# ScalarE held to the written order where an encoder's gates get their first two combinations

## The chip, the cores and the metric

The kernel runs on one core of a Trainium2 chip. The metric is device time in microseconds of one execution; less is better. The engines are named as in the profile: PE (TensorE, the matmuls; PEld is its weight load), DVE (VectorE), ACT (ScalarE), POOL (GpSimd) and SP (SyncE), the last two mostly issuing DMAs here.

## What is computed

A bidirectional encoder trunk of two layers on 512 tokens of width 1024, in float32:

```
for l in range(2):
    x = x + 0.5 * swiglu(rms_norm(x), ffn1)
    h = rms_norm(x)
    q, k, v, uf, ga, gf = split(h @ w_in)
    y_na = neighbourhood_attention(q, k, v, rpb) @ w_na_out
    y_f  = real(fft2(uf per group)) @ w_f_out
    x = x + (sigmoid(ga + b0) * y_na + sigmoid(gf + b1) * y_f) @ w_o
    x = x + 0.5 * swiglu(rms_norm(x), ffn2)
return rms_norm(x)
```

The change lies in the mixer, where the products for the gates `ga` and `gf` begin.

## The kernel before

**Float32 out of two halves.** Every matrix is split into a high part `hi` (rounded by ACT) and a low part `lo` (what is left, by DVE). A product is then three matmuls: L280 takes `hi` of both sides, L281 and L282 one `lo` and one `hi` each. The helper `split` (L284 to L290) issues the ACT instruction (L286) and the DVE instruction (L287). Weights of 128x1024 float32 go through the same split, in `Item.prep`, into tiles `whi` and `wlo`, three buffers each; a weight that is needed with its sign turned is split at L172 (ACT) and L173 (DVE).

**The stream of weights.** All weights stand in one list in the order of their use. `ws.next()` hands out the next one, and first has those prepared that lie up to two further on; `ws.prep(n)` prepares up to place n. Their loads into `raw` tiles run eight items ahead, on SP's queue. In the gates some weights are sums of matrices: POOL's queue issues a DMA that adds a second matrix to a `raw` tile, at L152 ahead of the first use and at L179 between two uses.

**Seven products for eight.** A block of the gate products follows Strassen's scheme. `gate_block` runs the products in the order 1, 5, 2, 6, 7, 3, 4. Products 1, 6, 7 and 4 go to the PSUM pair `A`, 5 and 3 to `B`, 2 to `C`. The weight `d` serves products 5, 6 and 3, with another matrix added between them. On the side of the activations the products need combinations of the four quarters `B[i, j]` of the normalised input, which itself is held as `xh` and `xl`:

- `t1` = quarter (0,0) less (0,1), for product 5: `minus` (two subtractions, L1088, and an addition, L1089), then `split` into `t1h` (ACT) and `t1l` (DVE).
- `t2` = `t1` plus quarter (1,1), for product 6: two additions in place at L1097, then `split` into `t2h` and `t2l`.
- `third` and `fourth` make the two others later, while the gate products run; `fourth` changes the tile of `t1` again and writes into the second half of `xh` and `xl`.

**The section.** Ahead of the gate products stands the product of the attention's output `o` with its weights: `fill(o, ns, 0)` takes two weights, and for each of four blocks of 128 tokens it issues twelve matmuls into a PSUM bank `ps` (`rows_of`) and a copy to `fs` on ACT (L943). It is a generator, which yields after each block.

**What sets the order.** The kernel is written for a scheduler that orders each engine's instructions by itself. Inside `tc.manual_schedule(engines=...)` the named engines keep the order in which the code is written; the others stay free. Each engine then runs its own list strictly in that order, and a buffer that is still in use makes the instruction that wants it wait, with all that is queued behind it on its engine. Before the change the section names DVE alone. So DVE has, in this order: three weights' `wlo`, the three steps of `t1`, `t1l`, the two additions, `t2l`, and the `wlo` of the second gate weight (L173), which the `ws.next()` inside `fill` brings. The scheduler put ACT's `whi` of the second gate weight (L172) and of the third (L286) ahead of `t1h`, and the fourth ahead of `t2h`.

```
def split(hi, lo, src, scale=None):
    if scale is None:
        S.activation(hi, src, AF.Copy)
        V.tensor_tensor(lo, src, hi.bitcast(F32), ALU.subtract)
def parts(src, s):
    h, l = slot(F32R, s + "h"), slot(F32R, s + "l")
    split(h, l, src)
    return h, l, 0
```

Of the kernel before, what the change touches and what calls it, by code (L numbers as in the profile page):

```python
# [92 lines left out]
def encoder_kernel(  # L93
# [19 lines left out]
    def slot(dt=F32, s="k", shape=(4, 256)):  # L113
        return kp.tile([P, *shape], dt, tag="k", name=nm(s), bufs=23)
# [129 lines left out]
    class Stream:  # L244
# [25 lines left out]
        def next(self):  # L270
            self.prep(self.pos + 1 + AHEAD)
            it = self.items[self.pos]
            self.pos += 1
            return it.out

    ws = Stream()
# [149 lines left out]
# [4 lines that stand above are left out]
# [246 lines left out]
    def stage_mixer(l, norm, nxt):  # L676
# [15 lines left out]
        for hl in range(2):  # L692
            for c in range(2):
                G.dma_start(out=dfs[c][hl], in_=dft[hl, c])
            src = bass.AP(tensor=rot.tensor, offset=rot.offset + hl * T, ap=[[0, P], [1, T]])
# [121 lines left out]
        o, q, k, bms = [], {}, {}, {}  # L817
# [106 lines left out]
        def rows_of(src, tb, w):  # L924

            ps = bank()
            t = slice(tb * P, (tb + 1) * P)
            for kt, (h_, l_) in enumerate(src):
                wh, wl = w[kt // 2]
                c = slice((kt % 2) * T, (kt % 2 + 1) * T)  # L930
                mm3(ps, h_[:, t], l_[:, t], wh[:, c], wl[:, c], kt == 0, kt == 3)
            return ps

        fs, ns = {}, {}

        def fill(src, to, i):

            w = [ws.next(), ws.next()]
            for tb in range(TB):
                if tb % 2 == 0:  # L940
                    to[i, tb // 2] = slot(F32, "fs", (2, T))
                ps = rows_of(src, tb, w)
                S.activation(to[i, tb // 2][:, tb % 2, :], ps, AF.Copy)  # L943
                yield
# [116 lines left out]
        def f_rows():  # L1061
            for i in range(2):
                yield from fill(yf, fs, i)
# [11 lines left out]
        for which in range(2):  # L1075
            b_ = slot(F32, "gb", (D,))
            src = bass.AP(tensor=gbias.tensor, offset=gbias.offset + (2 * l + which) * D, ap=[[0, P], [1, D]])
# [7 lines left out]
        def minus(p, q, s):  # L1085
            t, u = slot(F32, s), slot(F32, s)
            for z, d in enumerate((t, u)):
                V.tensor_tensor(d, p[z], q[z], ALU.subtract)  # L1088
            V.tensor_tensor(t, t, u, ALU.add)  # L1089
            return t  # L1090

        with tc.manual_schedule(engines={mybir.EngineType.DVE}):
            ws.prep(ws.pos + 3)
            t12 = minus(B[0, 0], B[0, 1], "t1")
            acts[5] = parts(t12, "t1")
            for z in B[1, 1]:
                V.tensor_tensor(t12, t12, z, ALU.add)  # L1097
            acts[6] = parts(t12, "t2")
            n_fill = fill(o, ns, 0)
            next(n_fill)  # L1100
        for _ in n_fill:
            pass

        def third():
# [13 lines left out]
        w = [ws.next(), ws.next()]  # L1118
# [71 lines left out]
    for kt in range(DT):  # L1190
        src = slot(F32, "xt", (T,))
# [9 lines left out]
    for l in range(L):  # L1201
        nxt = Norm(3 * l + 1)
        stage_ffn(norm, nxt, False)
        norm, nxt = nxt, Norm(3 * l + 2)
        stage_mixer(l, norm, nxt)
        norm, nxt = nxt, Norm(3 * l + 3)
        stage_ffn(norm, nxt, l == L - 1)
        norm = nxt
# [130 lines left out]
```

## Time and profile before

| | |
|---|---|
| time, median of 3 runs | 1957.36 us (1956.55 to 1959.98) |
| the profiled execution | 1960.45 us, its span 1958.0 us |
| PE busy | 1918.9 us (98%) |
| PEld busy | 1585.9 us (81%) |
| DVE busy | 1616.4 us (83%) |
| ACT busy | 1121.0 us (57%) |
| POOL busy | 198.3 us (10%) |
| moved by DMA | 361.82 MB, mean 185 GB/s |

Times in the views count from the start of the span. Busy shares are means over stages with different limits, so what the section is worth is read from its own stretch: around 490 to 560 us in layer 0, and 1461 to 1530 us in layer 1. A row's text "out<-in" names the tiles; the number in square brackets is the idle time of the engine ahead of the instruction, with what ended it.

### The profile page before, as it was taken

How to read it: one execution, taken by the hardware profiler on the slowest of the kernel's cores; microseconds unless marked ns; L12 is line 12 of the kernel's file. 1: busy time of each engine (PE TensorE's matmuls, PEld its weight loads, DVE VectorE, ACT ScalarE, POOL GpSimd, SP SyncE). 2: the span in 40 equal slices, each digit the busy share in tenths (PEclk: the TensorE clock that was granted, in tenths of full speed). 3: DMA queues.
4: the chain of work that ended last, by engine and by line, in shares of the span. 5: the costliest groups of instructions: out<-in, count | busy, mean ns of one | idle time of the engine just before them, and what ended most of it. 6: DMA issues, size and time to landing. Idle time of an engine off the chain costs nothing.

```text
span 1958.0 us, 24573 instructions
## 1 busy us (share of the span) xinstructions
PE 1918.9 (98%) x8997; PEld 1585.9 (81%) x8997; DVE 1616.4 (83%) x1936; ACT 1121.0 (57%) x1594; POOL 198.3 (10%) x242
## 2 busy tenths in 40 slices
PE   8999999999899999999999999999998999999997
PEld 6888887888778888888788888878887888888885
DVE  7778899598779877889977878995877888787898
ACT  6555666455556655566555556653555666555663
POOL 0001010200111000101000100102101110010010
PEclk9999999999999999999999999999999999999999
DMA  8677499221997567749757765984039974776593
GB/s 293 186 201 193 147 264 321 72 61 58 239 221 203 133 188 204 185 152 262 226 141 194 198 177 167 278 267 114 18 103 231 238 185 134 207 183 172 172 282 121
DMA packets 105704, 361.82 MB, mean 185 GB/s; under 512 B 12016, under 2 KB 14192, under 8 KB 105584
## 3 DMA queue, kind: packets, MB, share of 16 engines
q1 hardware_dynamic: 78576, 266.92, 39.9%
q0 software_dynamic: 27008, 93.34, 26.2%
q8 instruction: 70, 1.15, 0.2%
q14 instruction: 50, 0.41, 0.1%
HBM read 354.97 MB, written 2.10 MB: 182 GB/s over the span
## 4 chain that ended last, share of the span: by engine, by line
PE 83%; DVE 10%; DMA 3%; issue 2%; ACT 2%; SPq 0%; DVEq 0%; POOL 0%; ACTq 0%; POOLq 0%
PE A L281 8%; PE A L282 8%; PE A L280 8%; PE o L281 5%; PE o L282 5%; PE o L280 5%; PE B L281 4%; PE B L282 4%; PE B L280 4%; PE ps L281 4%; PE ps L282 4%; PE ps L280 4%; DVE wlo L287 3%; DMA raw<-in_wst_dram 2%; PE C L281 2%
## 5 line engine op out<-in xcount | busy, mean ns | idle before, releaser
L287 DVE TENSOR_TENSOR wlo<-raw,whi 128x1024 fp32r<-128x1024 f32 (+1 forms) x522 | 620.9, 1196 | 259.2 <-ACT whi L286 258.0
L286 ACT ACTIVATE whi<-raw 128x1024 fp32r<-128x1024 f32 (+1 forms) x522 | 540.4, 1038 | 513.8 <-PE A L282 130.2
L152 POOL DMA_DIRECT2D raw<-in_wst_dram x152 | 131.2, 874 | 1343.3 <-DMA raw<-in_wst_dram 898.1
L281 PE MATMUL A<-wlo,xh 128*128 128x512 f32 x384 | 152.0, 396 | 12.9 <-DVE wlo L173 12.4
L170 DVE TENSOR_TENSOR raw<-raw,raw 128x1024 f32<-128x1024 f32 (+1 forms) x128 | 150.9, 1189 | 2.4
L282 PE MATMUL A<-whi,xl 128*128 128x512 f32 x384 | 151.2, 394 | 0.0
L280 PE MATMUL A<-whi,xh 128*128 128x512 f32 x384 | 150.0, 392 | 0.4 <-ACT whi L172 0.4
L172 ACT ACTIVATE whi<-raw 128x1024 fp32r<-128x1024 f32 x76 | 78.8, 1038 | 85.7 <-PE B L282 33.2
L173 DVE SCALAR_TENSOR_TENSOR wlo<-raw,whi 128x1024 fp32r<-128x1024 f32 x76 | 89.8, 1193 | 13.5 <-ACT whi L172 13.5
L281 PEld LDWEIGHTS A<-wlo,xh 128*128 128x128 f32 x384 | 73.1, 190 | 30.2 <-DVE wlo L173 14.1
L436 ACT ACTIVATE sn<-A 128x512 f32<-128x512 f32 x96 | 57.3, 598 | 52.1 <-PE A L282 52.0
L282 PEld LDWEIGHTS A<-whi,xl 128*128 128x128 f32 x384 | 73.2, 191 | 15.1
L280 PEld LDWEIGHTS A<-whi,xh 128*128 128x128 f32 x384 | 72.6, 189 | 15.9 <-ACT whi L172 0.8
L281 PE MATMUL B<-wlo,t1h 128*128 128x512 f32 x192 | 75.4, 393 | 1.3 <-DVE wlo L287 1.2
L280 PE MATMUL B<-whi,t1h 128*128 128x512 f32 x192 | 76.1, 398 | 0.1
L280 PE MATMUL A<-whi,t2h 128*128 128x512 f32 x192 | 75.1, 391 | 0.0
L282 PE MATMUL B<-whi,t1l 128*128 128x512 f32 x192 | 75.1, 391 | 0.0
L280 PE MATMUL C<-whi,xh 128*128 128x512 f32 x192 | 75.0, 390 | 0.0
L280 PE MATMUL A<-whi,t3h 128*128 128x512 f32 x192 | 74.9, 390 | 0.0
L281 PE MATMUL C<-wlo,xh 128*128 128x512 f32 x192 | 74.8, 390 | 0.0
L281 PE MATMUL A<-wlo,t3h 128*128 128x512 f32 x192 | 74.7, 389 | 0.0
L281 PE MATMUL A<-wlo,t2h 128*128 128x512 f32 x192 | 74.7, 389 | 0.0
(336 smaller groups left out, 4917.8 us busy)
## 6 DMA issues: line engine op xcount, KB each, us to landing
raw<-in_wst_dram SPq DMA_DIRECT2D x462, 512.0 KB
raw<-in_wst_dram POOLq DMA_DIRECT2D x168, 512.0 KB, 7.8
raw<-in_wst_dram SPq DMA_DIRECT2D x32, 256.0 KB
vs<-v SPq DMA_DIRECT2D x12, 256.0 KB
bw<-in_rpb_dram SPq DMA_DIRECT2D x32, 68.0 KB
xt<-in_xtr_dram SPq DMA_DIRECT2D x8, 256.0 KB
x<-in_xin_dram SPq DMA_DIRECT2D x4, 512.0 KB
raw<-in_wst_dram POOLq DMA_DIRECT2D x8, 256.0 KB, 9.2
```

Source lines behind the costliest of these rows:

```text
L152: G.dma_start(out=self.t, in_=wst[GRAN_AT[self.plus]][:, 0 : self.n], accum_op=ALU.add)
L170: V.tensor_tensor(t, t, self.add.t, ALU.add)
L172: S.activation(hi, t, AF.Copy, scale=-1.0)
L173: V.scalar_tensor_tensor(lo, t, -1.0, hi.bitcast(F32), ALU.mult, ALU.subtract)
L280: PE.matmul(ps, lh, rh, start=start, stop=False, skip_group_check=again)
L281: PE.matmul(ps, lh, rl, start=False, stop=False, skip_group_check=again)
L282: PE.matmul(ps, ll, rh, start=False, stop=stop, skip_group_check=again)
L286: S.activation(hi, src, AF.Copy)
L287: V.tensor_tensor(lo, src, hi.bitcast(F32), ALU.subtract)
L436: S.activation(t[:, b, :], ps[b], AF.Copy)
```

## The change

The section names ACT beside DVE, so ACT's instructions there keep the written order too. The first block's matmuls and copy of `fill` leave the section, and with them go the other three; its two weights are still taken inside it, and handed to `fill`.

```diff
-        def fill(src, to, i):
-
-            w = [ws.next(), ws.next()]
+        def fill(src, to, i, w=None):
+
+            w = w or [ws.next(), ws.next()]
             for tb in range(TB):
...
-        with tc.manual_schedule(engines={mybir.EngineType.DVE}):
+        with tc.manual_schedule(engines={mybir.EngineType.DVE, mybir.EngineType.Activation}):
             ws.prep(ws.pos + 3)
             t12 = minus(B[0, 0], B[0, 1], "t1")
             acts[5] = parts(t12, "t1")
             for z in B[1, 1]:
                 V.tensor_tensor(t12, t12, z, ALU.add)
             acts[6] = parts(t12, "t2")
-            n_fill = fill(o, ns, 0)
-            next(n_fill)
-        for _ in n_fill:
+            w = [ws.next(), ws.next()]
+        for _ in fill(o, ns, 0, w):
             pass
```

## The prediction, made before the result was known

> **What bounds the kernel now.** I read the page first (PE is busy for 98% of the span), then the waits of the stretch from 500 to 640 us, which holds the changed section of layer 0, then the order of time of ACT, DVE and PE there. Each layer runs the section once, and layer 1 repeats layer 0 at 971.29 us later (the difference of two PE rows below, 1484.90 and 513.61).
>
> The waits (engine, line, what it waited for; total us, times, longest):
>
> ```profile
> DVE wlo L287 <- ACT whi L286: 16.4, 10, 4.0
> ...
> ACT whi L172 <- issue: 7.9, 1, 7.9
> ...
> DVE t1l L287 <- ACT t1h L286: 6.5, 1, 6.5
> ...
> PE A L281 <- DVE wlo L173: 6.0, 2, 5.7
> ```
>
> The last row is what counts: PE stands for 5.7 us for one `wlo`. ACT, then DVE, then PE in order of time (start, length, ..., idle before and its releaser):
>
> ```profile
> 494.03 1.05 ACT L172 ACTIVATE whi<-raw 128x1024 fp32r<-128x1024 f32 x1
> 502.98 1.06 ACT L172 ACTIVATE whi<-raw 128x1024 fp32r<-128x1024 f32 x1 [7.90 <-issue]
> 504.29 1.06 ACT L286 ACTIVATE whi<-raw 128x1024 fp32r<-128x1024 f32 x1 [0.25 <-PE ps L282]
> 505.26 1.04 ACT L286 ACTIVATE t1h<-t 128x1024 fp32r<-128x1024 f32 x1
> ...
> 510.11 1.06 ACT L286 ACTIVATE t2h<-t 128x1024 fp32r<-128x1024 f32 x1 [1.99 <-DVE t L1097]
> 511.07 2.04 ACT L943 ACTIVATE fs<-ps 128x512 f32<-128x512 f32 x4
> ...
> 539.79 2.01 ACT L286 ACTIVATE whi<-raw 128x1024 fp32r<-128x1024 f32 x2 [4.20 <-DMA raw<-in_wst_dram]
> ```
>
> ```profile
> 498.65 1.22 DVE L1089 TENSOR_TENSOR t<-t,t 128x1024 f32<-128x1024 f32 x1
> 506.33 1.23 DVE L287 TENSOR_TENSOR t1l<-t,t1h 128x1024 fp32r<-128x1024 f32 x1 [6.46 <-ACT t1h L286]
> ...
> 511.20 1.23 DVE L287 TENSOR_TENSOR t2l<-t,t2h 128x1024 fp32r<-128x1024 f32 x1 [1.12 <-ACT t2h L286]
> 512.34 1.22 DVE L173 SCALAR_TENSOR_TENSOR wlo<-raw,whi 128x1024 fp32r<-128x1024 f32 x1
> 513.48 2.35 DVE L287 TENSOR_TENSOR wlo<-raw,whi 128x1024 fp32r<-128x1024 f32 x2
> ...
> 540.88 1.23 DVE L287 TENSOR_TENSOR wlo<-raw,whi 128x1024 fp32r<-128x1024 f32 x1 [4.03 <-ACT whi L286]
> ```
>
> ```profile
> 506.81 0.62 PE L280 MATMUL A<-whi,xh 128*128 128x512 f32 x2
> 507.27 0.61 PE L280 MATMUL B<-whi,t1h 128*128 128x512 f32 x2
> 513.61 0.79 PE L281 MATMUL A<-wlo,xh 128*128 128x512 f32 x1 [5.73 <-DVE wlo L173]
> ...
> 517.96 0.39 PE L281 MATMUL B<-wlo,t1h 128*128 128x512 f32 x1
> ...
> 522.97 0.39 PE L280 MATMUL C<-whi,xh 128*128 128x512 f32 x1
> ...
> 528.63 0.39 PE L281 MATMUL A<-wlo,t2h 128*128 128x512 f32 x1
> ...
> 542.40 0.39 PE L281 MATMUL B<-wlo,xh 128*128 128x512 f32 x1
> ...
> 545.82 0.50 PE L281 MATMUL A<-wlo,xh 128*128 128x512 f32 x1 [0.53 <-DVE wlo L287]
> ```
>
> DVE has the first combination at 498.65 + 1.22 = 499.87, and ACT is idle then, yet `t1h` starts at 505.26. ACT's queue has two weight splits ahead of it: the `whi` at 502.98 waits for a free buffer until PE has used it up, and the one at 504.29 does too. DVE, held to the written order, stands 6.46 us at `t1l`; behind that stand the two additions, `t2l`, and only then the `wlo` that PE wants at about 507.9. The second half of that price is the clock, told by these stretches (busy us and instructions of PE, PEld, DVE, ACT, POOL, then granted PE clock, DMA share, GB/s):
>
> ```profile
> 511.01:517.83 6.82, 4.22 (x10) 3.35 (x11) 6.63 (x6) 2.70 (x6) 1.71 (x2) 0.50 0.74 159
> 517.83:524.66 6.83, 6.83 (x31) 5.64 (x31) 6.83 (x7) 5.71 (x7) 0.00 (x0) 1.00 0.86 171
> 524.66:539.69 15.03, 15.03 (x68) 12.21 (x67) 10.99 (x12) 6.87 (x9) 2.60 (x3) 1.00 0.94 246
> 1483.80:1490.63 6.83, 5.73 (x14) 4.48 (x15) 6.83 (x7) 2.25 (x5) 1.70 (x2) 0.50 0.72 152
> 954.74:958.15 3.41, 0.95 (x3) 0.30 (x2) 3.41 (x5) 3.02 (x4) 0.00 (x0) 1.00 0.59 171
> 958.15:961.57 3.42, 3.36 (x8) 2.68 (x9) 3.42 (x5) 1.49 (x3) 0.00 (x0) 0.50 0.88 293
> ```
>
> After the stall the clock is at half for 6.82 us in either layer. From 513.61 to 517.96 PE issues ten matmuls, 0.435 us each; from 517.96 to 522.97 twenty-two, 0.228 us each.
>
> **The change part by part.** It adds and removes no instruction; it fixes ACT's order in the section. The order that the program of the changed kernel has, engine by engine: ACT does `whi` of the first gate weight (494.03), `t1h`, `t2h`, then `whi` of the second (502.98 before), the four `fs` copies, and the two `whi` of B's weights. DVE keeps its order up to the second gate weight's `wlo`, then takes the two steps of `fourth` ahead of B's two `wlo`. PE does B's first two matmuls after all of A instead of ahead of A's last ten. SP's and POOL's orders are as before, so no DMA passes another.
>
> *The chain to A's last weight, layer 0.* `t1h` starts on DVE's release: 499.90 (a hand-over between the two engines takes 0.03 us: 505.26 + 1.04 to 506.33). That is 5.36 us earlier. From there the same work at the same lengths: `t1l` 506.33 - 5.36 = 500.97, `t2h` 504.75, `t2l` 505.84, `wlo` 506.98. The `whi` that it needs is now the late one: it stands behind `t2h`, starts 0.96 us after it (511.07 - 510.11) at 505.71 instead of 502.98, and ends at 506.77. PE wants it at 506.81, so its delay of 2.73 us costs nothing, but with 0.04 us of cover; each us that `t2h` came later would cost PE one. PE's `wlo` matmul follows the `wlo` by 513.61 - 512.34 = 1.27 us: 508.25, against 513.61.
>
> *A's rest and B.* Ten matmuls of A at 0.228 us end at 510.53, if the clock stays whole; two of B follow, to 510.99. B's first `wlo` now has two steps of DVE ahead of it at 1.14 us each (512.34 to 513.48 is such a step): 506.98 + 3 x 1.14 = 510.40, usable at 511.67. Its `whi` comes after the four `fs` copies, 506.67 + 2.04 = 508.71 to 509.77, in time. So a new, smaller wait of 0.68 us stands there; the second `wlo` (usable at 512.81) is early for 513.95. B's other 22 matmuls take 5.02 us, and C starts at 516.69 against 522.97: **6.28 us** earlier in layer 0. In the split of it, 5.36 comes from the wait and the rest, 0.92, from the whole clock less the new wait and the two matmuls that moved behind.
>
> Layer 1, PE and then DVE:
>
> ```profile
> 1484.90 0.79 PE L281 MATMUL A<-wlo,xh 128*128 128x512 f32 x1 [5.73 <-DVE wlo L173]
> ...
> 1494.96 0.39 PE L280 MATMUL C<-whi,xh 128*128 128x512 f32 x1
> ...
> 1514.43 0.39 PE L281 MATMUL B<-wlo,xh 128*128 128x512 f32 x1
> ```
>
> ```profile
> 1510.62 1.23 DVE L287 TENSOR_TENSOR wlo<-raw,whi 128x1024 fp32r<-128x1024 f32 x1 [1.78 <-ACT whi L286]
> ```
>
> There C started at 1494.96, which is 523.67 on layer 0's scale, because the half clock covered more matmuls; against 516.69 the gain is **6.98 us**.
>
> *Does C find its weights?* DVE goes on without a hole: two `wlo` of B, two steps of `third`, then C's `wlo` at 510.40 + 4 x 1.14 = 514.96, usable at 516.23; C wants it at 516.69 + 2 x 0.228 = 517.15. The cover is 0.9 us.
>
> *What is late next: the weights made by adding DMAs.* `d` is used three times in a block, and between the uses POOL's queue adds another matrix to it.
>
> ```profile
> 515.22 0.85 POOL L179 DMA_DIRECT2D raw<-in_wst_dram  x1 [7.05 <-DVE wlo L287]
> ...
> 529.27 1.22 POOL L179 DMA_DIRECT2D raw<-in_wst_dram  x1
> ```
>
> In layer 0 the last of these additions, issued at 529.27, held ACT 4.20 us until 539.79 and made the `wlo` at 540.88 (done 542.11) for the matmul at 542.40: 0.29 us of cover. PE now wants it 6.28 us earlier. How much earlier it lands is unknown; bounds: if issue and landing follow DVE's shift, 5.36 us; if only the DMA engines' idle time can be filled, 0.26 x 6.82 + 0.14 x 6.83 + 0.06 x 15.03 = 3.6 us (the first three stretches above). With 5.36 the layer keeps 5.36 + 0.29 = 5.65 us, with 3.6 it keeps 3.9. I take the middle, 4.5 us earlier, so 4.8 us kept. In layer 1 the same `wlo` is done at 1511.85 for 1514.43, a cover of 2.58 us: with 4.5 us all 6.98 are kept, with 3.6 it is 6.2.
>
> **Sum:** 4.8 + 7.0 = 11.8 us. The profiled execution took 1960.45 us (span 1958.0 and 2.45 around it), so it would take 1948.6; the median of the runs, 1957.36, becomes 1945.6 (0.60% less). PE is the bound behind the section (`cl` of the next stage follows it), so the rest of the kernel only shifts.
>
> **A rule that speaks against it.** In the trace one stretch of 3.41 us with PE busy for 0.95 of it (954.74) is followed by half clock for 3.42 us. The changed section has two short holes, from about 507.4 to 508.25 and from 511.1 to 511.67, so any stretch of 3.41 us has at most 1.4 us of idle time, 2.0 us busy. The Trainium skill, "TensorE: Matmul & The Clock Gate", Part 1: the HAM clock gate, has the clock halved after an idle window of about 3.4 us; by it the holes are harmless and 1945.6 stands, though the trace's row at 954.74 shows that a window need not be wholly idle. The same page, under "A second HAM failure mode", tells of a kernel whose frequent micro-idles between groups of matmuls made the clock swing; by that the time would be the first rival's.
>
> **The rivals.**
> 1. *The clock falls all the same.* The two holes, 0.57 us of work between them and the next, drop it for 6.82 us in each layer with PE at work: 2 x 6.82 / 2 = 6.8 us lost, gain 5.0, 1952.4. Against it: 2.0 us busy of 3.41 is twice the 954.74 stretch's share. Chance 0.06.
> 2. *DMA is the bound.* The added matrices land when they landed before. Layer 0 keeps nothing (PE waits for 542.11 as before), layer 1 keeps its cover of 2.58 us: 1954.8. For it: the share of 0.94 ahead of 539.69. Against it: 0.74 and 0.86 in the stretches ahead, idle because the requests that free buffers and finished `wlo` send were late too. Chance 0.09.
> 3. *Slower: an addition blocks ACT.* In the new order `whi` of the second use of `d` stands ahead of `t3h` and of B's `sn` copies. Its addition was issued 515.22 - 513.48 = 1.74 us after the start of the `wlo`, so now at 512.14; from `whi` to a usable `wlo` takes 542.11 - 539.79 = 2.32 us. It costs the whole gain and more if it lands later than 528.63 - 2.32 = 526.31, that is 14.2 us after its issue. The slow addition above took 539.79 - 529.27 = 10.5 us. At 16 us PE would lose 1.8 us against before in each layer: 1961.0. Chance 0.05.
>
> That the change does not do what it says is excluded by the program's own order.
>
> **How the numbers follow.** About 0.2% (3.9 us) can be told from no change. The forecast has 0.80: its own range is 1943.6 (layer 0's addition lands in time, 6.28 + 6.98 us, and the wait of 0.53 us at 545.82, which the late `wlo` left behind, goes too) to 1950.9 (half of the idle DMA time is filled, 1.8 us: layer 0 keeps 2.1, layer 1 4.4). That is the range given; what it leaves out is the three rivals, 0.20. Faster by over 0.2%: forecast and first rival, 0.86; within: second, 0.09; slower: third, 0.05.
>
> **What would show it.** `t1h` within 0.1 us of L1089's end; `t1l`'s wait of 6.46 us down to about 1.1; PE's wait for `wlo` L173 down from 5.73 to under 1 us, a new one of about 0.7 for B's first `wlo`; no half clock between 505 and 525 or 1476 and 1496; C 6 to 7 us earlier against the section's last L1089. In layer 0 a wait of PE or ACT near the addition's landing, with C's gain cut to about 5 us there. Wrong it would be if PE's next wait after C took back more than 4 us in both layers, if half clock stayed, or if `whi` came to PE later than the `wlo`.

## The result, and the profile after

The changed kernel takes 1950.53 us (median of 6 runs, 1949.48 to 1952.34), the kernel before 1957.71 us beside it (6 runs). The ratio is 0.9961, with a 95% interval of 0.9948 to 0.9974: 7.2 us less, where 11.8 were forecast. The forecast of 1945.6 was 4.9 us too low; the range, 1943.6 to 1950.9, holds the result near its upper end. The profiled execution took 1950.02 us, its span 1948.1.

The section does what the prediction said. ACT in order of time, with the columns of before (start, length, idle before and its releaser):

```profile
500.11 1.06 ACT L286 ACTIVATE t1h<-t 128x1024 fp32r<-128x1024 f32 x1 [4.88 <-DVE t L1089]
504.99 1.06 ACT L286 ACTIVATE t2h<-t 128x1024 fp32r<-128x1024 f32 x1 [3.81 <-DVE t L1097]
505.96 1.04 ACT L172 ACTIVATE whi<-raw 128x1024 fp32r<-128x1024 f32 x1
506.90 2.04 ACT L943 ACTIVATE fs<-ps 128x512 f32<-128x512 f32 x4
...
519.69 1.06 ACT L286 ACTIVATE whi<-raw 128x1024 fp32r<-128x1024 f32 x1 [3.40 <-DMA raw<-in_wst_dram]
...
523.82 2.96 ACT L286 ACTIVATE whi<-raw 128x1024 fp32r<-128x1024 f32 x3 [1.15 <-DMA raw<-in_wst_dram]
528.81 1.06 ACT L958 ACTIVATE sn<-sn 128x1024 f32<-128x1024 f32 x1 [2.04 <-DVE sn L954]
529.77 1.07 ACT L436 ACTIVATE sn<-A 128x512 f32<-128x512 f32 x2
```

`t1h` now starts as soon as DVE's L1089 has ended. DVE:

```profile
498.80 1.23 DVE L1089 TENSOR_TENSOR t<-t,t 128x1024 f32<-128x1024 f32 x1
501.21 1.23 DVE L287 TENSOR_TENSOR t1l<-t,t1h 128x1024 fp32r<-128x1024 f32 x1 [1.19 <-ACT t1h L286]
...
507.23 1.22 DVE L173 SCALAR_TENSOR_TENSOR wlo<-raw,whi 128x1024 fp32r<-128x1024 f32 x1
...
515.29 1.22 DVE L287 TENSOR_TENSOR wlo<-raw,whi 128x1024 fp32r<-128x1024 f32 x1
...
524.91 1.23 DVE L287 TENSOR_TENSOR wlo<-raw,whi 128x1024 fp32r<-128x1024 f32 x1 [0.63 <-ACT whi L286]
526.17 1.29 DVE L441 TENSOR_TENSOR sn<-C,sn 128x512 f32<-128x512 f32 x2
527.37 1.41 DVE L954 SCALAR_TENSOR_TENSOR sn<-sn,r,gb 128x512 f32<-128x512 f32 x2
```

The wait at `t1l` fell from 6.46 to 1.19 us. PE, with all its waits up to product 7:

```profile
508.50 0.50 PE L281 MATMUL A<-wlo,xh 128*128 128x512 f32 x1 [0.71 <-DVE wlo L173]
...
512.03 0.50 PE L281 MATMUL B<-wlo,t1h 128*128 128x512 f32 x1 [0.51 <-DVE wlo L287]
...
517.16 0.39 PE L280 MATMUL C<-whi,xh 128*128 128x512 f32 x1
517.39 0.39 PE L281 MATMUL C<-wlo,xh 128*128 128x512 f32 x1
...
526.19 0.50 PE L281 MATMUL A<-wlo,t2h 128*128 128x512 f32 x1 [0.48 <-DVE wlo L287]
...
530.40 0.50 PE L280 MATMUL A<-whi,t3h 128*128 128x512 f32 x1 [1.42 <-ACT sn L436]
```

The wait of 5.73 us is 0.71, the new one at B 0.51. The last two rows are what the prediction did not have: product 6 waits for its second `wlo`, and product 7 for ACT's `sn` copies, which free the pair `A`. The clock, by stretches (length, busy us of PE, PEld, DVE, ACT and POOL, then granted clock, DMA share, GB/s; as the view counts it, the share can pass 1):

```profile
507.00:510.41 3.41, 2.70 (x11) 1.91 (x11) 3.38 (x4) 3.41 (x6) 0.82 (x1) 1.00 1.07 213
510.41:513.82 3.41, 2.90 (x13) 2.06 (x13) 3.41 (x4) 2.35 (x4) 1.27 (x2) 1.00 0.99 259
...
505.00:525.00 20.00, 18.78 (x81) 14.64 (x80) 16.25 (x15) 13.94 (x19) 4.26 (x5) 1.00 0.95 238
...
1470.00:1490.00 20.00, 18.77 (x81) 14.66 (x80) 17.25 (x15) 14.73 (x19) 4.26 (x5) 1.00 0.98 253
```

There is no half clock, though both short holes lie in these stretches. In the kernel before, the clock in 505 to 525 was 0.83 and the DMA share 0.85; the share is 0.95 now.

**Marks.** To compare kernels I count from A's first matmul in each layer (504.24 and 1469.21 here; 504.09 and 1475.38 before), layer 0 and layer 1, in us:

| profile | C starts | product 7 starts | `cl` of the next stage |
|---|---|---|---|
| before | 18.87, 19.59 | 29.78, 30.49 | 140.71, 139.60 |
| after | 12.93, 12.91 | 26.17, 25.11 | 135.22, 135.94 |

So C came 5.94 and 6.68 us earlier, product 7 only 3.61 and 5.38, and the next stage 5.49 and 3.66.

### The profile page after: what moved, and what is told of

It is laid out like the page before. It is cut to its first block, busy times and chain, and to the rows that moved or that the text cites. A ratio compares the mean times of both kernels' runs of the same rounds, so it can differ in the third digit from the quotient of the medians.

```text
span 1948.1 us, 24569 instructions
## 1 busy us (share of the span) xinstructions
PE 1914.3 (98%) x8997; PEld 1580.8 (81%) x8997; DVE 1616.7 (83%) x1936; ACT 1120.2 (58%) x1594; POOL 198.6 (10%) x242
## 3 DMA queue, kind: packets, MB, share of 16 engines
q8 instruction: 70, 1.15, 0.2%
## 4 chain that ended last, share of the span: by engine, by line
PE 78%; DVE 11%; DMA 5%; issue 4%; ACT 2%; POOL 0%; SPq 0%; DVEq 0%; ACTq 0%; POOLq 0%
PE A L280 8%; PE A L282 8%; PE A L281 8%; PE o L281 4%; PE o L280 4%; PE o L282 4%; PE B L281 4%; DMA raw<-in_wst_dram 4%; PE B L282 4%; PE B L280 4%; PE ps L281 4%; PE ps L282 4%; PE ps L280 4%; DVE wlo L287 3%; PE C L281 2%
## 5 line engine op out<-in xcount | busy, mean ns | idle before, releaser
L170 DVE TENSOR_TENSOR raw<-raw,raw 128x1024 f32<-128x1024 f32 (+1 forms) x128 | 150.9, 1189 | 2.4
L282 PE MATMUL A<-whi,t2l 128*128 128x512 f32 x192 | 74.7, 389 | 0.0
```

Of the source, the lines that this page charges most:

```text
L170: V.tensor_tensor(t, t, self.add.t, ALU.add)
L282: PE.matmul(ps, ll, rh, start=False, stop=stop, skip_group_check=again)
```

## Experiments

**Both kernels again, and without the suspected additions (four kernels on one chip, where the kernel before took 1956.92).** Between products 5 and 6 a DMA of POOL's queue (L179) adds `a` to `d`; that is the second use of `d`. Two kernels leave it out in the first gate block (two DMAs a layer) and keep the order of all else:

```diff
-                        add(d, then=a.key if dma else None)
+                        add(d, then=a.key if dma and (name("d"), idx) != ("gd", 0) else None)
```

> The kernel before, unchanged, run and profiled once more. All theories: ratio 1.000 within 0.2%. The clock theory (the half clock after the stall of 5.7 us depends on where the stall falls among the windows of the clock, so it costs more in some executions than in others): this profile has its half-clock stretches in other places or lengths than the first one (6.82 us in each layer's section and 3.42 us at 958), its runs differ by 2 to 4 us, and the runs with the lower mean clock are the longer ones. Its rival (the first profile stands for all executions): half-clock stretches of the same length in both sections again, and a span within 1 us of 1958.0.

> The changed kernel, timed in more rounds and profiled once more. The giving-back theory (C starts 6.0 and 6.7 us earlier in the two layers; then the weight of product 6 that a DMA is adding to lands late, DVE stands at its wlo, the tanh and the copies of the next A wait behind that, and PE stands about 1.6 us at product 7): ratio 0.9955 to 0.9970, PE's wait ahead of product 7 between 1.2 and 2 us in both layers again. A theory of chance (the late landing was of that one execution): the wait is absent in at least one layer.

> The kernel before without the same two DMAs a layer; it leaves the same addition out. Giving-back theory: before the change these additions were hidden by the stall, so this is at most 2 us faster than before (the small waits of 0.7 and 0.4 us in layer 0 may go), and the changed kernel gains 10 to 13 us on it once both are without the additions. Rival (the additions cost DMA time in any order): it gains as much as the changed kernel does from leaving them out, 3 to 6 us.

> The changed kernel without the DMA that adds a matrix to d between products 5 and 6 of the first gate block (two DMAs a layer); it leaves that addition out of the computation. Nothing else moves in any engine's order. Giving-back theory: whi of product 6 no longer waits for a landing, PE's waits at product 6's second half and at product 7 (0.64 and 1.58 us in layer 0, 1.3 in layer 1) shrink to under 0.4 us, and it is 3 to 6 us faster than the changed kernel. Order rival (the new order of ACT, xh and whi ahead of t3h and of B's copies, makes the wait at product 7 by itself): that wait stays above 1.2 us, and the gain is under 2 us.

| kernel | median us | ratio to before (95%) | C | product 7 | `cl` |
|---|---|---|---|---|---|
| before again | 1957.74 | 1.0003 (0.9994 to 1.0012) | 19.34, 19.67 | no wait | 139.30, 139.68 |
| after again | 1948.67 | 0.9962 (0.9950 to 0.9975) | 12.92, 12.92 | 24.55, 25.40 | 133.67, 135.69 |
| before, without | 1957.46 | 1.0005 (0.9996 to 1.0014) | 18.62, 19.45 | 29.52, 30.36 | 138.60, 139.43 |
| after, without | 1945.42 | 0.9943 (0.9931 to 0.9956) | 12.92, 12.91 | 23.82, 23.82 | 133.30, 132.95 |

The kernel before, run again, bears out neither of its two theories whole. The half clock lasts 6.83 us in each section again (0.83 in 505 to 525 and in 1470 to 1490), but none stands between 950 and 965 (1.00, against 0.89 in the first profile), the span is 1954.6 us and not 1958.0, and PE has no wait behind product 7 in layer 0. The execution that the prediction was read from was thus one of the longer ones. The changed kernel again has a wait at product 7 in both layers, but in layer 0 it is 0.59 us, less than the 1.2 expected at the least.

In the old order the additions cost nothing that these runs can tell. In the new one they cost 3.25 us in the medians (3 to 6 were expected), though the intervals of 0.9962 and 0.9943 overlap slightly; the marks tell it more sharply. Without the additions product 7 starts at 23.82 in both layers, and PE's waits end with B's first `wlo`, layer 0:

```profile
508.27 0.50 PE L281 MATMUL A<-wlo,xh 128*128 128x512 f32 x1 [0.71 <-DVE wlo L173]
...
511.81 0.50 PE L281 MATMUL B<-wlo,t1h 128*128 128x512 f32 x1 [0.50 <-DVE wlo L287]
```

The change is then worth 12.0 us (1957.46 to 1945.42), about the 11.8 that were forecast. That the two agree so closely is in part chance: by layers `cl` comes 5.30 and 6.48 us earlier, against 4.8 and 7.0, and without these additions the last one for the third use lands earlier too (28.1 and 27.8 us behind A's first matmul, against 29.5 and 30.9 in the profile after), which the forecast did not count on.

**ACT's name alone.** `n_fill = fill(o, ns, 0)` and `next(n_fill)` stay in the section, as before; only `mybir.EngineType.Activation` is added. (Moving `fill` out alone gives the program of before, instruction for instruction.)

> One part of the change alone: ACT is named in the section, the first block of fill stays inside it. Theory (the two engines' order is all that the change does; handing the weights to fill does nothing): every engine's order is that of the changed kernel, so ratio 0.9950 to 0.9975 against before, C 12.9 us after A. Rival (the first block's copy, written into ACT's fixed order, holds it): C more than 13.5 us after A.

1951.15 us, 0.9948 (0.9934 to 0.9962), just below the 0.9950 to 0.9975 expected; C at 12.92 and 12.91, product 7 at 23.97 and 25.60. The engines' orders are those of the changed kernel: naming ACT is the whole change.

**Earlier additions (three kernels, on the chip of the last one, where the kernel before took 1960.44).** If the addition is late because it is issued late, issue it earlier. Each kernel prepares the weights sooner, and so sends POOL's request sooner:

```diff
# prep_d: behind w
             w = [ws.next(), ws.next()]
+            ws.prep(ws.pos + 4)
# w_first: the two weights ahead of t2's additions
             acts[5] = parts(t12, "t1")
+            w = [ws.next(), ws.next()]
...
-            w = [ws.next(), ws.next()]
# w_d_first: w_first, and
             w = [ws.next(), ws.next()]
+            ws.prep(ws.pos + 4)
```

> The changed kernel, and the two weights of product 5 are prepared inside the section too, so that their wlo stand ahead of the two steps of fourth on DVE. Giving-back theory: the DMAs that add to them are issued about 2.3 us earlier, PE's wait for B's first wlo (0.68) goes, C comes 12.2 us after A, and the wait at product 7 shrinks by 1 to 1.5 us: 2 to 4 us faster than the changed kernel in all. Rival (DMA bandwidth sets the landing, whatever the issue): C gains 0.7 us in either layer, the wait at product 7 grows by as much, no gain.

> The changed kernel with the second gate weight taken ahead of t2 instead of behind it, so that its whi and wlo stand ahead of t2's two additions. Theory: PE's wait for A's wlo (0.9 us a layer) goes, and B's wlo is early too; C comes 11.4 to 12 us after A (24 + 24 matmuls of 0.228 us are 10.9); the additions to d go out 2 us or more earlier, so product 7 waits less than 1 us: 3 to 6 us faster than the changed kernel. Rival (landing of the additions bound by DMA bandwidth): what C gains is lost at product 6 or 7, no gain.

> As the one before, with product 5's two weights ahead of t2 as well. Theory: the additions to d go out as early as B's weights allow (about 4 us earlier than in the changed kernel), no wait at products 6 and 7, C 11 to 11.5 us after A: 4 to 7 us faster than the changed kernel, 11 to 14 faster than before. Rival for it: t2 is now late, since t2h stands behind the whi that waits for A's first weight to be used up; then PE waits for t2 or the wait comes at product 7 again, and it is not faster than the one before.

None of the three is faster than the changed kernel, where 2 to 7 us were expected of them, and an earlier request did not bring the addition in time. They take 1954.7, 1954.67 and 1953.4 us (ratios 0.9966, 0.9966 and 0.9962): 2.3 to 3.6 us more than the changed kernel's order on that chip (1951.15), although C starts at 11.9, 10.9 and 10.9. ACT and PE of the kernel that takes the two weights first:

```profile
518.25 1.06 ACT L286 ACTIVATE whi<-raw 128x1024 fp32r<-128x1024 f32 x1 [1.83 <-DMA raw<-in_wst_dram]
522.04 1.06 ACT L286 ACTIVATE whi<-raw 128x1024 fp32r<-128x1024 f32 x1 [2.73 <-DMA raw<-in_wst_dram]
```

```profile
524.41 0.50 PE L281 MATMUL A<-wlo,t2h 128*128 128x512 f32 x1 [0.75 <-DVE wlo L287]
...
527.45 0.49 PE L280 MATMUL A<-whi,t3h 128*128 128x512 f32 x1 [0.20 <-ACT sn L436]
...
529.32 0.50 PE L281 MATMUL A<-wlo,t3h 128*128 128x512 f32 x1 [1.38 <-DVE wlo L287]
...
543.99 0.50 PE L281 MATMUL A<-wlo,xh 128*128 128x512 f32 x1 [1.59 <-DVE wlo L287]
```

The second `whi` still waits for the DMA until 522.04, counted from A's first matmul 1.6 us earlier than in the changed kernel. The second of the two additions was issued 6.0 us after A's first matmul in this kernel, 9.2 in the changed one and 12.3 before; it landed at 17.9 and 19.0 (layers 0 and 1), at 19.5 and 18.2, and at 19.1 and 19.0. Issue hardly moves the landing. That made the next four kernels: take the addition off the DMA, and see what the earlier C is worth without it.

**The addition on DVE, and C earlier without it (four kernels, another chip, before 1957.94).** In the first of them DVE adds `a` to `d` (L170), and all is computed:

```diff
-                        add(d, then=a.key if dma else None)
+                        add(d, then=a.key if dma and (name("d"), idx) != ("gd", 0) else None)
                     elif m == 6:
-                        add(d, None if dma else a, then=b.key if dma else None)
+                        add(d, a if not dma or (name("d"), idx) == ("gd", 0) else None, then=b.key if dma else None)
```

> The changed kernel, but the matrix `a` is added to `d` between products 5 and 6 of the first gate block by DVE (L170, from the `raw` tile of `a`, which then is kept four weights longer) and not by a DMA of POOL: four additions of DVE of about 1.2 us each in the kernel, four adding DMAs of 512 KB less. Everything is computed. Theory (the adding DMA's landing at 523.7 us is what gives back 1.5 us at product 7, and more behind it): no wait at product 7, `cl` about 133 to 134 us behind A's first matmul in each layer (changed kernel: 135.2 and 135.9), a median 2 to 4 us under the changed kernel's. Rival (DVE is what is short there; two more steps of 1.2 us a layer in front of `t3l` take its place): product 7 as late as in the changed kernel or later, no gain, up to 2.4 us a layer lost.

> As dve_add, and with the two weights of `fill` taken ahead of the two additions that make `t2`, so that PE's first `wlo` comes two steps of DVE earlier. Everything is computed. Theory: C starts at 10.9 us behind A (changed kernel 12.9), and as no adding DMA stands in the way 1 to 2 us of the two are kept in each layer: 2 to 4 us under dve_add. Rival (DVE is short): C 10.9 as well, but a wait at product 7 gives it back, the time of dve_add within 1 us or above it.

> The kernel with the two weights taken ahead of `t2`'s additions (C 10.9 us behind A, 2 us earlier than in the changed kernel, yet 3.5 us slower in all), and without the DMA that adds `a` to `d` between products 5 and 6 of the first gate block (left out: that addition, two DMAs a layer). If the adding DMA is what it loses by: no wait at product 7, the time 2 to 4 us under the changed kernel without the addition (1945.4), so 1941.5 to 1943.5. If its loss is DVE's own or `t2h`'s place: still 2 us or more above the changed kernel without the addition, 1947 or more.

> The changed kernel again, on the chip of these runs, for the comparison: 0.996 of the kernel before, 1948.5 to 1951.5 us; C 12.9 us behind A in each layer, PE's wait at product 7 between 0.7 and 2.4 us.

| kernel | median us | ratio to before (95%) | C | product 7 | `cl` |
|---|---|---|---|---|---|
| the changed kernel, a third time | 1950.60 | 0.9956 (0.9944 to 0.9969) | 12.95, 12.91 | 23.85, 25.70 | 136.13, 135.51 |
| DVE adds | 1949.10 | 0.9949 (0.9936 to 0.9961) | 12.91, 12.95 | 24.27, 24.30 | 135.39, 136.47 |
| DVE adds, two weights first | 1951.43 | 0.9966 (0.9955 to 0.9977) | 10.88, 10.88 | 22.76, 22.73 | 136.79, 135.65 |
| two weights first, no addition | 1943.37 | 0.9921 (0.9906 to 0.9935) | 10.88, 10.88 | 21.76, 21.76 | 132.16, 132.65 |

The last row hits its expectation: 1943.37 against 1941.5 to 1943.5. With the additions the same order took 0.9966 of before, without them 0.9921: 0.0045 of 1958 is 8.8 us. So in these three orders, the earlier PE gets to product 6, the more the additions cost: nothing before, some 3 us in the changed kernel, 9 us with C another 2 us earlier.

DVE's addition does not give the expected 2 to 4 us. Product 7 starts only 0.5 us late in both layers, near what the theory had, but the next stage comes no sooner; 1949.10 and 1950.60 cannot be told apart. DVE and PE in layer 0:

```profile
518.18 1.22 DVE L170 TENSOR_TENSOR raw<-raw,raw 128x1024 f32<-128x1024 f32 x1
519.32 1.22 DVE L287 TENSOR_TENSOR t3l<-t,t3h 128x1024 fp32r<-128x1024 f32 x1
520.45 1.22 DVE L170 TENSOR_TENSOR raw<-raw,raw 128x1024 f32<-128x1024 f32 x1
521.59 1.22 DVE L287 TENSOR_TENSOR wlo<-raw,whi 128x1024 fp32r<-128x1024 f32 x1
```

```profile
522.87 0.50 PE L281 MATMUL A<-wlo,t2h 128*128 128x512 f32 x1 [0.18 <-DVE wlo L287]
...
539.42 0.50 PE L281 MATMUL A<-wlo,xh 128*128 128x512 f32 x1 [0.15 <-DVE wlo L287]
...
545.44 0.50 PE L281 MATMUL A<-wlo,xh 128*128 128x512 f32 x1 [0.28 <-DVE wlo L173]
```

Now DVE has no hole from 516 to 531 us, and PE runs into `wlo` after `wlo` with no cover. That DVE is what is short is not shown by itself, though. The two additions for the third use, still DMAs, are asked for later (19.4 and 21.2 us behind A's first matmul, against 16.0 and 19.4 in the changed kernel without the additions). The last of them lands at 29.6 and 30.1 in the two layers, and ACT and then DVE wait for it; in layer 0:

```profile
533.39 2.01 ACT L286 ACTIVATE whi<-raw 128x1024 fp32r<-128x1024 f32 x2 [2.10 <-DMA raw<-in_wst_dram]
...
534.49 1.23 DVE L287 TENSOR_TENSOR wlo<-raw,whi 128x1024 fp32r<-128x1024 f32 x1 [1.93 <-ACT whi L286]
```

On ACT the scheduler also put `t3h` and B's `sn` copies ahead of the first of the second use's two `whi` here, so product 7's shorter wait need not be the addition's doing alone. How much each part counts for, these runs do not separate. With the two weights first it is worse: in that kernel PE waits 1.33 us for a `wlo` at product 4 (540.23), and nothing is left of the 2 us by which C comes earlier. No kernel that computes everything was shown to beat the changed one.

**What the changed kernel loses at product 7.** Four profiles of its order give eight passes. The second addition for the second use is issued 9.2 us after A's first matmul in all eight; it lands at different times, and the start of product 7 beyond 23.82 follows it:

| landed, us after A's first matmul | 16.0 | 16.5 | 17.4 | 18.2 | 18.7 | 18.7 | 19.0 | 19.5 |
|---|---|---|---|---|---|---|---|---|
| product 7 late by, us | 0.03 | 0.15 | 0.73 | 1.29 | 1.58 | 1.78 | 1.88 | 2.35 |
| lost behind product 7, us | 3.2 | 1.6 | 0.0 | 1.7 | 1.2 | 2.7 | 0.7 | 0.0 |

The rows of the profile after show the chain: the landing releases `whi` at 523.82, that the `wlo` at 524.91; behind it in DVE's list stand L441 and L954, on L954 waits ACT's L958, and behind L958 stand the copies that free the pair `A`, which product 7 wants. In layer 0 the mean of the four is 0.8 us, in layer 1 1.6 us.

The rest is lost behind product 7: the last row of the table is the time from product 7 to `cl` beyond 109.1 us, which a pass without waits takes. It comes to 1.2 us in layer 0 and 1.6 in layer 1 on the mean, at least as much as the loss at product 7, and it does not follow the landing: the pass with the earliest has the most of it. In the third run of the changed kernel the second use was in time in layer 0 (landed 16.0; a wait of 0.7 to 2.4 us at product 7 was expected), and the addition for the third use was late; ACT and PE:

```profile
534.82 2.01 ACT L286 ACTIVATE whi<-raw 128x1024 fp32r<-128x1024 f32 x2 [5.33 <-DMA raw<-in_wst_dram]
```

```profile
537.19 0.50 PE L281 MATMUL B<-wlo,xh 128*128 128x512 f32 x1 [0.71 <-DVE wlo L287]
...
540.85 0.50 PE L281 MATMUL A<-wlo,xh 128*128 128x512 f32 x1 [0.65 <-DVE wlo L287]
```

For this pass the third use is shown as the cause. In the other passes that lost time PE's waits behind product 7 stand at product 4, in the first products of the second gate block and, in two passes, at that block's product 7; how much of them goes back to the third use was not tested.

## Why the prediction came out as it did

*The chain to A's last weight: right.* `t1h` starts 0.08 us behind L1089's end (498.80 + 1.23 = 500.03), the wait at `t1l` is 1.19 (said: about 1.1), `whi` of the second gate weight starts at 505.96 and costs nothing, and PE's `wlo` matmul is at 508.50; 508.25 was said, on a time base that is 0.15 earlier.

*A's rest and B: right.* The new wait for B's first `wlo` is 0.51 us of idle time; against the slot in which that matmul was due (511.36, it starts at 512.03) it is 0.67, and 0.68 was said. C's gain, means of three profiles in the old order (before, again, and without the additions, which cost nothing there) against four in the new, is 6.0 us in layer 0 and 6.7 in layer 1 (said 6.28 and 6.98).

*C's weights: right, with a slip.* C's `wlo` ends at 515.29 + 1.22 = 516.51 for a matmul at 517.39: 0.88 us of cover, 0.9 was said. The prediction let C want it two matmuls of 0.228 us behind its first; it is one (517.16 to 517.39), so its own terms give 0.7, and both the `wlo` and C came a little later than said.

*The clock, rival 1: it stays whole* in both layers of all four profiles in the new order (1.00 in 505 to 525 and 1470 to 1490). By the rule of the Trainium skill, "TensorE: Matmul & The Clock Gate", Part 1: the HAM clock gate, that it takes an idle window of about 3.4 us to halve the clock, the holes are harmless, and the trace agrees: stretches of 3.41 us with PE busy for 2.70 and 2.90 keep a clock of 1.00 (how idle a window must be, no run here shows: the row at 954.74, busy for 0.95 us, was not wholly idle and was followed by half clock). The swing that the page describes under "A second HAM failure mode" did not come.

*What is late next: the failed step.* It costed the third use of `d` alone. There the size was right: the late addition lands 29.9 us after A's first matmul (mean of the eight passes) against 34.3 in the old order (mean of four), 4.4 us earlier, and 4.5 was taken (by layers it is 5.3 and 3.5). But the second use has such an addition too, and the step took for granted that it would keep up with C. It did not: issued 3.1 us earlier, it landed 1.0 us earlier (18.0 against 19.0, the same means), while PE wanted it 6.0 and 6.7 us earlier. What hid it before can be read in a row of the kernel before that the prediction left aside:

```profile
525.88 1.06 ACT L286 ACTIVATE whi<-raw 128x1024 fp32r<-128x1024 f32 x1 [0.52 <-PE C L282]
```

This `whi` waited for PE to free a buffer, not for the landing at 523.15 (by the trace), 2.7 us ahead of it; its `wlo` lay 3.0 us ahead of PE (528.32 to 531.35). The cover was 5.7 us, less than C moved.

The sum's terms, by `cl`, the same means: layer 0 was given 4.8 and kept 4.62 us, part of the loss standing at another addition than the one that was costed; layer 1 was given all of 7.0 and kept 3.45. The mis-sized term is layer 1's: it had 2.58 us of cover at the third use, and the second use, which the term passed over, cost it 1.6 us at product 7 and the later waits 1.6 more. That layer 0 comes out near its term is luck in part: the cover of 0.29 us was that of one execution. In the two other profiles of the old order PE has no wait behind product 7 in layer 0, and `cl` stands at 139.30 and 138.60, not at 140.71. Luck, too, has its share in the result's lying inside the range: the range's slow end stands for less idle DMA time filled at the third use, and nothing in it allows for the second. 4.62 + 3.45 is 8.1 us; the medians of the changed order give 7.2, 8.3 and 7.3 beside those of before on their chips, and 9.3 with ACT's name alone.

*Rivals 2 and 3.* Rival 2 had the mechanism for the second use (the addition lands about when it landed before) but looked for it at the third. Rival 3 had the place: `whi` of the second use stands ahead of `t3h` and B's `sn` copies, and ACT did wait there, 3.40 and 1.15 us. It priced only the point at which the kernel would get slower than before (14.2 us from issue to landing; 7.3 and 10.3 were measured) and nothing short of it, where the gain is eaten up. One mechanism, costed at one use and only as a catastrophe at the other, is how 3.7 us went missing.

The Trainium skill, "DMA: Bandwidth & Descriptors", under "Issuing engines are not separate DMA queues", says that transfers issued by SP, ACT and POOL all run on the same 16 DMA engines. The trace agrees with it here: with a DMA share of 0.95 to 1.04 over 505 to 525 us in the new order's four profiles, an earlier request on POOL's queue did not buy an earlier landing of the same size. Whether the engines' share or the order within POOL's own queue holds the landing back, no run here separates.

## What to carry to other kernels

When a stage starts earlier, go through every later use of every buffer that a transfer refills, not only the one that waits now: count its cover from the landing, not from the instruction that follows, and move the landing by what the transfers in flight allow, not by what the request does. An engine that keeps a written order passes a late landing on to whatever stands behind it; here the waiting weight split held a copy that freed a PSUM pair, one product later. And once an engine takes over a transfer's work, check what that engine has left: DVE's 2.4 us a layer closed the holes in its list, and the gain was gone, though the runs do not show that this alone took it. Read the cover from more than one execution, too.

## What the runs showed of the hardware

An adding DMA took 5.0 us at the least, issue to landing, when no other of its kind was in flight; over a whole execution such ones took 6.8 to 7.3 us in the median and up to 11.0, so most are not at that least. In the changed order four of 512 KB are asked for within 7.7 to 8.7 us and the last took 6.8 to 10.3 us; with the two weights first, four within 4.7 to 5.7 us, the last took 11.9 to 12.9. In the profile after they land 7.1, 10.7, 15.3 and 19.5 us behind A's first matmul, 3.7 to 4.6 us apart. With the same issue (9.2 us) the last of them lands anywhere from 16.0 to 19.5 us, by execution and layer; product 7 follows it (0.03 to 2.35 us late), the passes' `cl` does not, as 0.0 to 3.2 us are lost behind product 7 besides.
